# Feed-forward groups of four, a braided first tile, and a chained closing in a macaron decoder step

## The chip, the core and the metric

The kernel runs on one core of a Trainium2 chip. The metric is the device time of one execution in microseconds; a comparison uses the median of several. The kernel is written for TensorE (PE, the matrix array), VectorE (DVE), ScalarE (ACT) and SyncE (SP, which issues nearly all loads and stores); a scheduler fixes the order of the instructions on each engine beforehand, and each engine works through its own row in that order.

## What is computed

One decoder layer for 1024 prompt tokens and 64 sampled tokens, 1024 wide, all in 32-bit floats: a half-step SwiGLU block, two mixers side by side, and a second half-step SwiGLU block.

```python
def swiglu_ffn(x, w_up, w_down):
    gate, up = jnp.split(x @ w_up, 2, axis=-1)
    return (jax.nn.silu(gate) * up) @ w_down          # inner width 2816

x = x + 0.5 * rms_norm(swiglu_ffn(rms_norm(x, n1), up1, down1), n1_post)
m = parallel_mixers(rms_norm(x, mix_norm_pre), w_in, ...)   # windowed attention and gated DeltaNet
x = x + rms_norm(m, mix_norm_post)
x = x + 0.5 * rms_norm(swiglu_ffn(rms_norm(x, n2), up2, down2), n2_post)
```

## The kernel before

Activations lie transposed: 1024 features as 8 slices (k) of 128 partitions, the 1088 tokens along the free axis in chunks of 384, 384 and 320 (chunk 0, 1, 2). Every matmul with full precision is made of three, from a high and a low half of each operand: `hi*xh + hi*xl + lo*xh` (`gemm`, lines 133 to 142). So each loaded weight, 128 x 512 in a staging buffer `raw` (4 of them), is split: ACT casts the high half (line 111), DVE subtracts it (line 112).

A feed-forward part (class `FFN`, lines 307 to 505) goes over 22 inner tiles. Chunk 2 is done plainly: `one` makes gate and up of one tile (48 matmuls) and their gated product `h`. Chunks 0 and 1 are done together by a seven-product scheme with combinations of the halves of weights (`factors`) and of inputs (`combine`): `two` makes one inner tile for both chunks with 84 matmuls of 384 columns. The inputs' pieces are `ch` and `cl`, eleven steps of `combine`, each with a 128 x 1536 subtraction on DVE (lines 261, 269).

Inner tiles come in groups of two (`G = 2`, 11 groups). When a group's tiles are done, its down products are due: for each of the 8 output slices `down_k` sums six matmuls in PSUM and adds them into `y` (DVE, line 334; for group 0 a copy by ACT, line 332). They are put behind the next group's first tile (`pay`). A down weight is loaded as two half rows of one inner tile, 4 loads a group.

The order of a part is `run`: chunk 2's first groups (pass A, 5 groups in the first part, 7 in the second), chunks 0 and 1 whole (pass B), chunk 2's other groups (6 and 4). Work of VectorE and ScalarE is spread over pass A in small steps: `take(early, 3)` after each tile makes the input of pass B (loads, sum of squares `rms`, scaling, `combine`), `take(late, 3)` the closing of chunks 0 and 1. Closing a chunk (`close1`): `post` (sum of squares over y, scaling, residual), the mixers' input xn2 (`xb`), and the sum for its norm `r2`. Each sum over partitions is one matmul with a matrix of ones into `po` (line 172), followed by a reciprocal square root on ACT (line 173) and a Newton step on ACT and DVE (lines 145 to 147).

The first group multiplies unnormed x (`xu`) and takes the norm scale r into its gated product; from the second group on the operand is the scaled `xs` (`make_xnr`). At the end chunk 2 is closed while the mixers' first units (k, v, four q) run on chunks 0 and 1: `do_kv` and `do_q` evict into slabs `SL` that lie in a pool over the feed-forward part's.

Of the kernel before, what the change touches and what calls it, by code (L numbers as in the profile page):

```python
# [13 lines left out]
P = 128  # L14
# [21 lines left out]
def body(ctx: ExitStack, tc: tile.TileContext, d):  # L36
# [84 lines left out]
    def load_w(src, name, each=None, pool=wp, tag="w"):  # L121

        r = []
        for i in range(2):
            t = raw(f"{name}_{i}")
            nc.sync.dma_start(t, src[:, 4 * i : 4 * i + 4, :])
            if each:
                each(i)
            r.append(split_w(t, *slot(f"{name}_{i}", pool, tag)))
        return r  # L130

    def gemm(ps, w, xs, c, ks=range(KT)):
# [3 lines left out]
        for i, k in enumerate(ks):  # L136
            hi, lo = w[k // 4]
            j = k % 4
            first, last = i == 0, i == len(ks) - 1
            nc.tensor.matmul(ps[:, :n], hi[:, j, :], at(xh, k), start=first, stop=False)  # L140
            nc.tensor.matmul(ps[:, :n], hi[:, j, :], at(xl, k), start=False, stop=False)  # L141
            nc.tensor.matmul(ps[:, :n], lo[:, j, :], at(xh, k), start=False, stop=last)  # L142
# [11 lines left out]
    def po_tile():  # L154
        return pp.tile([P, 512], F32, tag="po", name=uid("po"), bufs=1)

    def rms(pool, src, n, dst, scale, urgent=False):
# [13 lines left out]
        with tc.high_priority(offset=4000 if urgent else 0):  # L171
            nc.tensor.matmul(ps[:, :n], ones, one, start=True, stop=True)
# [122 lines left out]
    CUT1, CUT2 = 5, 7  # L295
    G = 2
    NG = NFF // G

# [9 lines left out]
    class FFN:  # L308


        def __init__(self, up, down, pool, tag):
            self.up, self.down, self.pool, self.tag = up, down, pool, tag
            self.y = [None] * 3
            self.due = None

        def ldd(self, f):
            src = self.down[f].rearrange("p (k m) -> p k m", m=P)
            return load_w(src, uid(f"d{self.tag}"), pool=self.pool, tag="d")

        def down_k(self, g, hs, wd, c, k):  # L320
# [14 lines left out]

        def pay(self):
            if self.due:
                self.due()
                self.due = None

        def one(self, hh, hl, wg, wu, xs, r):
# [3 lines left out]
            gemm(pg, wg, {c: xs}, c)  # L345
            gemm(pu, wu, {c: xs}, c)
# [12 lines left out]
        def pass_a(self, gs, xs, r=None, first=None, between=None):  # L359
# [3 lines left out]
            for g in gs:  # L363
                h = self.pool.tile([P, 4, width(2)], F32R, tag="big", name=f"h{self.tag}{g}")
                hs = [(h[:, 2 * i, :], h[:, 2 * i + 1, :]) for i in range(G)]
                ws = first() if first and g == 0 else None
                for i in range(G):
                    f = g * G + i
                    wg, wu = ws[i] if ws else [load_w(self.up[w * NFF + f], uid(f"u{self.tag}")) for w in range(2)]
                    self.one(*hs[i], wg, wu, xs(g), r(g) if r else None)  # L370
# [4 lines left out]

                def due(g=g, hs=hs):
                    wd = [self.ldd(g * G + i) for i in range(G)]
                    for k in range(KT):
                        self.down_k(g, hs, wd, 2, k)
                    between(g, G)  # L380

                self.due = due
# [13 lines left out]
        def factors(self, f):  # L396
# [3 lines left out]
            turn = [0]  # L400

            def full(name, src=None):
                turn[0] += 1
                t = raw(f"{n}_{name}") if turn[0] % 2 else self.pool.tile([P, 4, P], F32, tag="aq", name=f"{n}_{name}", bufs=3)
# [70 lines left out]
        def pass_b(self, cx, between):  # L475
            for g in range(NG):
                hs = []
                for i in range(G):
                    hs.append(self.two(g * G + i, cx))
                    self.pay()  # L480
                    if g == 0 and i == 0:
# [51 lines left out]
    with tc.tile_pool(name="f1", bufs=12, side="left", reuse_waits="tile") as big1, tc.tile_pool(  # L533
# [71 lines left out]
        def before(g, i):  # L605
            if g >= 1:
                take(early, 3)
# [869 lines left out]
```

## Time and profile before

| what | value |
|---|---|
| median of 3 runs (lowest to highest) | 2494.36 us (2488.65 to 2501.92) |
| profiled execution, its own time | 2494.16 us |
| its span | 2492.4 us |
| PE busy | 2415.2 us (97%), 14654 instructions |
| DVE busy | 1857.0 us (75%), 3770 instructions |
| ACT busy | 1145.1 us (46%), 2310 instructions |
| mean of the clock granted to PE | 0.988 |
| moved by DMA | 258.00 MB, mean 104 GB/s |

The profile is of one execution. The span is the time between its first and last instruction; a little of the run's time lies outside it. PE's busy time counts matmuls whose ends are modelled and which overlap, so that the distance from start to start tells its pace, not the duration in a row. PEclk is the clock granted to the array as a share of full speed; it has two levels, 1.0 (2.4 GHz) and 0.5 (1.2 GHz), and a number between them is a mean over a stretch.

### The profile page before, as it was taken

How to read it: one execution, taken by the hardware profiler on the slowest of the kernel's cores; microseconds unless marked ns; L12 is line 12 of the kernel's file. 1: busy time of each engine (PE TensorE's matmuls, PEld its weight loads, DVE VectorE, ACT ScalarE, POOL GpSimd, SP SyncE). 2: the span in 40 equal slices, each digit the busy share in tenths (PEclk: the TensorE clock that was granted, in tenths of full speed). 3: DMA queues.
4: the chain of work that ended last, by engine and by line, in shares of the span. 5: the costliest groups of instructions: out<-in, count | busy, mean ns of one | idle time of the engine just before them, and what ended most of it. 6: DMA issues, size and time to landing. Idle time of an engine off the chain costs nothing.

```text
span 2492.4 us, 39425 instructions
## 1 busy us (share of the span) xinstructions
PE 2415.2 (97%) x14654; PEld 2315.4 (93%) x14654; DVE 1857.0 (75%) x3770; ACT 1145.1 (46%) x2310; POOL 49.3 (2%) x36
## 2 busy tenths in 40 slices
PE   7889999999999899999999999999998999999997
PEld 7889999999998876898889889999998999999997
DVE  6896787787898476798687735664998687777787
ACT  6644333332565278644545333255754333333353
POOL 0000000000000000001011100000000000000000
PEclk9999999999999999999999999999999999999998
DMA  6421221221554111222112335444542121221263
GB/s 222 143 95 64 73 73 59 77 69 60 185 199 161 64 52 34 87 70 78 61 59 74 105 107 159 138 146 149 192 151 89 64 77 64 72 73 60 98 209 129
DMA packets 157457, 258.00 MB, mean 104 GB/s; under 512 B 34544, under 2 KB 61616, under 8 KB 157256
## 3 DMA queue, kind: packets, MB, share of 16 engines
q1 hardware_dynamic: 157264, 255.47, 31.2%
q8 instruction: 115, 1.88, 0.3%
q14 instruction: 78, 0.64, 0.1%
HBM read 219.43 MB, written 36.96 MB: 103 GB/s over the span
## 4 chain that ended last, share of the span: by engine, by line
PE 83%; DVE 9%; ACT 3%; DMA 3%; issue 2%; SPq 0%; DVEq 0%; ACTq 0%
PE pa L141 10%; PE pa L140 10%; PE pa L142 10%; PE pa L440 8%; PE pa L441 8%; PE pa L439 8%; PE py L328 3%; PE ph L328 3%; PE py L329 3%; PE py L330 3%; PE ph L329 3%; PE ph L330 3%; DVE t L935 1%; PE po L848 1%; DVE s L1113 1%
## 5 line engine op out<-in xcount | busy, mean ns | idle before, releaser
L440 PE MATMUL pa<-cl,h_c_s 128*128 128x384 f32 x704 | 237.6, 338 | 9.2 <-DVE cl L269 9.2
L439 PE MATMUL pa<-ch,h_c_s 128*128 128x384 f32 x704 | 236.9, 337 | 2.6 <-ACT ch L268 2.5
L441 PE MATMUL pa<-ch,l_c_s 128*128 128x384 f32 x704 | 236.9, 337 | 0.0
L445 DVE TENSOR_TENSOR t<-pa,t 128x384 f32<-128x384 f32 x308 | 168.5, 553 | 44.4 <-PE pa L441 43.6
L440 PE MATMUL pa<-cl,h_c_a 128*128 128x384 f32 x528 | 176.7, 335 | 3.2 <-DVE cl L269 3.2
L439 PE MATMUL pa<-ch,h_c_a 128*128 128x384 f32 x528 | 176.8, 335 | 0.0
L441 PE MATMUL pa<-ch,l_c_a 128*128 128x384 f32 x528 | 176.6, 334 | 0.0
L440 PEld LDWEIGHTS pa<-cl,h_c_s 128*128 128x128 f32 x704 | 133.9, 190 | 9.9 <-DVE cl L269 9.9
L439 PEld LDWEIGHTS pa<-ch,h_c_s 128*128 128x128 f32 x704 | 133.4, 190 | 3.4 <-ACT ch L268 3.0
L441 PEld LDWEIGHTS pa<-ch,l_c_s 128*128 128x128 f32 x704 | 133.8, 190 | 0.0
L111 ACT CAST h_c_a<-r_c_a 128x512 fp32r<-128x512 f32 x132 | 81.9, 620 | 109.1 <-PE pa L440 88.9
L111 ACT CAST h_db<-r_db 128x512 fp32r<-128x512 f32 x88 | 52.9, 621 | 171.0 <-PE ph L329 113.1
L140 PE MATMUL pa<-xbh,h_ga 128*128 128x384 f32 (+1 forms) x384 | 129.2, 337 | 0.0
L141 PE MATMUL pa<-xbl,h_ga 128*128 128x384 f32 (+1 forms) x384 | 129.0, 336 | 0.0
L142 PE MATMUL pa<-xbh,l_ga 128*128 128x384 f32 (+1 forms) x384 | 128.5, 335 | 0.0
L111 ACT CAST h_da<-r_da 128x512 fp32r<-128x512 f32 x88 | 53.1, 620 | 157.6 <-PE ph L329 100.6
L111 ACT CAST h_c_s<-c_s 128x512 fp32r<-128x512 f32 x132 | 81.6, 618 | 62.3 <-PE pa L440 56.7
L328 PE MATMUL py<-ha,h_da 128*128 128x384 f32 (+1 forms) x264 | 88.3, 335 | 17.0 <-ACT ha L188 9.0
L440 PEld LDWEIGHTS pa<-cl,h_c_a 128*128 128x128 f32 x528 | 99.1, 188 | 3.7 <-DVE cl L269 3.7
L439 PEld LDWEIGHTS pa<-ch,h_c_a 128*128 128x128 f32 x528 | 99.1, 188 | 0.2
L441 PEld LDWEIGHTS pa<-ch,l_c_a 128*128 128x128 f32 x528 | 99.1, 188 | 0.0
L141 PE MATMUL pa<-xbl,h_qkv 128*128 128x384 f32 (+1 forms) x288 | 97.9, 340 | 0.0
(585 smaller groups left out, 7601.3 us busy)
## 6 DMA issues: line engine op xcount, KB each, us to landing
r_c_a<-in_up_dram SPq DMA_DIRECT2D x132, 256.0 KB
r_da<-in_dn_dram SPq DMA_DIRECT2D x88, 256.0 KB
r_ub<-in_up_dram SPq DMA_DIRECT2D x88, 256.0 KB
r_db<-in_dn_dram SPq DMA_DIRECT2D x88, 256.0 KB
r_ua<-in_up_dram SPq DMA_DIRECT2D x80, 256.0 KB
c_a<-in_up_dram SPq DMA_DIRECT2D x44, 256.0 KB
r_ga<-in_win_dram SPq DMA_DIRECT2D x32, 256.0 KB
r_wo<-in_wo_dram SPq DMA_DIRECT2D x32, 256.0 KB
```

Source lines behind the costliest of these rows:

```text
L111: nc.scalar.copy(hi, full)
L140: nc.tensor.matmul(ps[:, :n], hi[:, j, :], at(xh, k), start=first, stop=False)
L141: nc.tensor.matmul(ps[:, :n], hi[:, j, :], at(xl, k), start=False, stop=False)
L142: nc.tensor.matmul(ps[:, :n], lo[:, j, :], at(xh, k), start=False, stop=last)
L328: nc.tensor.matmul(ps[:, :n], hi[:, j, :], hh, start=i == 0, stop=False)
L329: nc.tensor.matmul(ps[:, :n], hi[:, j, :], hl, start=False, stop=False)
L330: nc.tensor.matmul(ps[:, :n], lo[:, j, :], hh, start=False, stop=i == G - 1)
L439: nc.tensor.matmul(ps, wh[:, k, :], xh[:, k, :], start=k == 0, stop=False)
L440: nc.tensor.matmul(ps, wh[:, k, :], xl[:, k, :], start=False, stop=False)
L441: nc.tensor.matmul(ps, wl[:, k, :], xh[:, k, :], start=False, stop=k == 3)
L445: nc.vector.tensor_tensor(out=out, in0=ps, in1=other, op=ALU.add)
L848: nc.tensor.matmul(po[hs, tp2 * 256 : tp2 * 256 + 256], vtok[:, blk * P + hs.start : blk * P + hs.stop], ptb[:, g2 * 512 + h2 * 256 : g2 * ...
```

## The change

Groups. `GROUPS` are four tiles each (4, 4, 4, 4, 4, 2) and pass A's first stage is three groups (12 tiles) in both parts. The down weights are laid out by output slice, `[k, partition, inner tile, 128]`, so one load of 256 KB holds the four tiles of a group for one k. A group's down products are two parts of four slices each (`owe`), one behind the first tile of the next group and one behind the second (`pay`); a product sums twelve matmuls. Weights of `one` and the down weights take staging buffers by turns from `raw` and from the pool `aq` of three that `factors` had used. `take` is 3 and 3 in the first part, 4 and 2 in the second.

Start. The first tile's gate and up alternate by k (`braid`), its four weight loads alternate with the four loads of x, its sum of squares gets a high priority, and the load of `wab` (the mixers' small weights) moves behind the first part.

Closing. The units' order is k, q, q, q, q, v; their slabs come from a pool of their own (`s2c`); and the two ones matmuls of chunk 2's closing get an ordering dependency (no wait) behind the chunk-1 products of the first and the fourth unit in number (u = 0 and 3).

```diff
-    CUT1, CUT2 = 5, 7
-    G = 2
-    NG = NFF // G
+    GROUPS = [range(f, min(f + 4, NFF)) for f in range(0, NFF, 4)]
+    CUT = 3
...
+        def raw(self, name):
+            self.turn += 1
+            if self.turn % 2:
+                return raw(name)
+            return self.pool.tile([P, 4, P], F32, tag="aq", name=f"q_{name}", bufs=3)
...
+        def ldd(self, g, k):
+            fs = GROUPS[g]
+            n = uid(f"d{self.tag}")
+            s = slice(0, len(fs))
+            t = self.raw(n)
+            nc.sync.dma_start(t[:, s, :], self.down[k][:, fs[0] : fs[-1] + 1, :])
+            hi, lo = slot(n, self.pool, "d")
+            return split_w(t[:, s, :], hi[:, s, :], lo[:, s, :])
...
-            for i in range(G):
-                hi, lo = wd[i][k // 4]
-                hh, hl = hs[i]
-                j = k % 4
-                nc.tensor.matmul(ps[:, :n], hi[:, j, :], hh, start=i == 0, stop=False)
-                nc.tensor.matmul(ps[:, :n], hi[:, j, :], hl, start=False, stop=False)
-                nc.tensor.matmul(ps[:, :n], lo[:, j, :], hh, start=False, stop=i == G - 1)
+            hi, lo = wd
+            for i, (hh, hl) in enumerate(hs):
+                nc.tensor.matmul(ps[:, :n], hi[:, i, :], hh, start=i == 0, stop=False)
+                nc.tensor.matmul(ps[:, :n], hi[:, i, :], hl, start=False, stop=False)
+                nc.tensor.matmul(ps[:, :n], lo[:, i, :], hh, start=False, stop=i == len(hs) - 1)
...
+        def owe(self, g, cs, hs, between):
+            def part(j):
+                for k in range(4 * j, 4 * j + 4):
+                    wd = self.ldd(g, k)
+                    for c in cs:
+                        self.down_k(g, [t[c] for t in hs], wd, c, k)
+                between(g, 4 + j)
+            self.due += [lambda: part(0), lambda: part(1)]
...
-            gemm(pg, wg, {c: xs}, c)
-            gemm(pu, wu, {c: xs}, c)
+            if braid:
+                for k in range(KT):
+                    for ps, w in ((pg, wg), (pu, wu)):
+                        gemm(ps, w, {c: xs}, c, ks=(k,), ends=(k == 0, k == KT - 1))
...
         def first():
...
+            for i in range(2):
+                for w in range(2):
+                    t = raw(f"w0{w}{i}")
+                    nc.sync.dma_start(t, d["up1"][w * NFF][:, 4 * i : 4 * i + 4, :])
+                    load_x(2, 4 * i + 2 * w)
+                    ws.append(split_w(t, *slot(f"w0{w}{i}")))
             nc.sync.dma_start(eye1, d["eye1"])
             drain(make_xn(x0[2], xu, V_N1A))
-            drain(stat(2))
+            with tc.high_priority(offset=20000):
+                drain(stat(2))
...
         drain(close1(2))
+        behind = sums[-2:]
...
-    SL = [(s2a if k < 11 else s2b).tile([P, NT], F32, tag=f"s{k}", name=f"s{k}") for k in range(16)]
+    SL = [(s2c if k in (0, 2, 3, 4, 5) else s2a).tile([P, NT], F32, tag=f"s{k}", name=f"s{k}") for k in range(16)]
...
-        for u in range(6):
+        for u in (0, 2, 3, 4, 5, 1):
...
+                if c == 1 and u in (0, 3):
+                    tc.add_manual_dep(behind[u // 3].ins, mm.ins.name, NOSYNC, reason="behind products that are ready")
...
-        take(early, 3)
-        if (g, i) == (CUT2 - 1, G - 1):
+        take(early, 4)
+        if (g, i) == (CUT - 1, 3):
             drain(early)
...
-    f2.run(CUT2, lambda g: xn3[0], cx2, lambda: again(xd[2], hn2, r3[2]), before, lambda g, i: take(late, 3))
+    f2.run(lambda g: xn3[0], cx2, lambda: again(xd[2], hn2, r3[2]), before, lambda g, i: (g, i) != (CUT, 0) and take(late, 2))
...
-        arr["dn" + n] = np.ascontiguousarray(L0(a + "_w_down")).reshape(NFF, P, 1024)
+        arr["dn" + n] = np.ascontiguousarray(L0(a + "_w_down").reshape(NFF, P, KT, P).transpose(2, 1, 0, 3))
```

How the order moves, at three places. PE at the start, before: the last products of the second tile (its up half, in ph) and the first down products (py, ph), which need `ha`, the first group's gated product. The first down product is the array's 98th instruction.

```order
L140 MATMUL ph_285<-xuh_1_128,h_wu_1_222 128x320
L141 MATMUL ph_285<-xul_1_130,h_wu_1_222 128x320
L142 MATMUL ph_285<-xuh_1_128,l_wu_1_223 128x320
L328 MATMUL py_482<-ha_136,h_da_0_460 128x320
L328 MATMUL ph_490<-ha_136,h_da_0_460 128x320
L328 MATMUL py_498<-ha_136,h_da_0_460 128x320
```

After, the same place: in front of the first down product now stand four tiles, so that it is the 194th instruction and not the 98th.

```order
L138 MATMUL ph_457<-xuh_1_128,h_ua_1_452 128x320
L139 MATMUL ph_457<-xul_1_130,h_ua_1_452 128x320
L140 MATMUL ph_457<-xuh_1_128,l_ua_1_453 128x320
L343 MATMUL py_643<-ha_133,h_da_639 128x320
L344 MATMUL py_643<-ha_133,h_da_639 128x320
L345 MATMUL py_643<-ha_133,l_da_640 128x320
L343 MATMUL py_643<-ha_133,h_da_639 128x320
```

The down product reads the same `ha`, 96 matmuls later, and goes on in one accumulator where before it changed with each matmul. DVE at the end of pass A's first stage in the first part, before: cl are the low halves of the combined inputs, the L350 row is the last tile's gated product, the L445 row already belongs to pass B.

```order
L269 TENSOR_TENSOR cl_1364<-cf_1183,ch_1363 128x1536
L261 TENSOR_TENSOR cf_1377<-x_1_122,cf_1361 128x1536
L269 TENSOR_TENSOR cl_1371<-x_0_123,ch_1370 128x1536
L350 TENSOR_TENSOR t_113_1460<-pa_1411,t_113_1460 128x320
L269 TENSOR_TENSOR cl_1380<-cf_1361,ch_1379 128x1536
L189 TENSOR_TENSOR ha_1186<-t_113_1460,ha_1186 128x320
L269 TENSOR_TENSOR cl_1466<-x_1_122,ch_1465 128x1536
L445 TENSOR_TENSOR t_124_1559<-pa_1546,t_122_1544 128x384
```

After, L381 is the gated product of the tenth of twelve tiles, L435 and L112 prepare weights for pass B, and L349 adds down products:

```order
L272 TENSOR_TENSOR cl_1255<-cf_1082,ch_1254 128x1536
L435 TENSOR_TENSOR q_c_s_1634<-r_c_a_1632,r_c_s_1624 128x512
L272 TENSOR_TENSOR cl_1262<-x_0_123,ch_1261 128x1536
L264 TENSOR_TENSOR cf_1268<-x_1_122,cf_1252 128x1536
L272 TENSOR_TENSOR cl_1271<-cf_1252,ch_1270 128x1536
L112 TENSOR_TENSOR l_c_a_1629<-r_c_a_1620,h_c_a_1628 128x512
L381 TENSOR_TENSOR t_101_1351<-pa_1302,t_101_1351 128x320
L349 TENSOR_TENSOR ya_1_132<-py_1362,ya_1_132 128x320
L112 TENSOR_TENSOR l_c_s_1637<-r_c_s_1624,h_c_s_1636 128x512
L192 TENSOR_TENSOR ha_1085<-t_101_1351,ha_1085 128x320
```

Three cl stand ahead of the tenth tile's product, with two tiles to follow; before, two of the four shown stood behind the last tile's. PE at the closing, before: po is the sum for chunk 2's mixer norm, the products around it are those of the second unit (v).

```order
L140 MATMUL pa_8628<-xbh_1_7176,h_kvq_0_1_8624 128x384
L141 MATMUL pa_8628<-xbl_1_7178,h_kvq_0_1_8624 128x384
L142 MATMUL pa_8628<-xbh_1_7176,l_kvq_0_1_8625 128x384
L172 MATMUL po_8468<-rms_8455,eye_72 128x320
L140 MATMUL pa_8654<-xbh_0_7921,h_kvq_0_0_8618 128x384
L141 MATMUL pa_8654<-xbl_0_7923,h_kvq_0_0_8618 128x384
```

After, the same sum:

```order
L140 MATMUL pa_8573<-xbh_1_7314,l_kvq_0_1_8570 128x384
L138 MATMUL pa_8599<-xbh_0_8035,h_kvq_0_0_8563 128x384
L139 MATMUL pa_8599<-xbl_0_8037,h_kvq_0_0_8563 128x384
L175 MATMUL po_8279<-rms_8266,eye_72 128x320
L140 MATMUL pa_8599<-xbh_0_8035,l_kvq_0_0_8564 128x384
L138 MATMUL pa_8599<-xbh_0_8035,h_kvq_0_0_8563 128x384
```

It stands behind the chunk-1 products of the fifth unit in number, the fourth to be issued (a q), between matmuls of the following accumulator; the sum of chunk 2's post norm stands 125 rows ahead of it.

## Rows read from the trace of the kernel before

**Rows 1.** The page's head.

```profile
span 2492.4 us, 39425 instructions
```

**Rows 2.** A stretch: PE, PEld, DVE, ACT, POOL busy (instructions); clock, DMA share, GB/s.

```profile
550.00:600.00 50.00, 50.00 (x289) 50.00 (x288) 39.03 (x71) 17.70 (x33) 0.00 (x0) 1.00 0.23 75
```

**Rows 3.** Waits of PE: waiting line, awaited line, us in total, times, longest.

```profile
PE pa L440 <- DVE cl L269: 12.4, 4, 4.6
PE po L172 <- DVE rms L168: 9.2, 2, 6.4
PE py L328 <- ACT ha L188: 9.0, 2, 7.3
PE py L328 <- ACT h_da L111: 8.0, 1, 8.0
PE pa L140 <- ACT xuh L195: 6.4, 1, 6.4
PE pa L140 <- DVE s L661: 2.9, 1, 2.9
PE pa L439 <- ACT ch L268: 2.5, 2, 1.3
```

**Rows 4.** Stretches, as in Rows 2, behind the pause of the closing.

```profile
815.00:820.00 5.00, 1.88 (x3) 0.97 (x4) 2.04 (x6) 2.79 (x5) 0.00 (x0) 0.50 0.00 0
820.00:830.00 10.00, 10.00 (x47) 9.25 (x47) 3.77 (x21) 1.24 (x2) 0.00 (x0) 0.79 0.14 50
```

**Rows 5.** Time line of PE: start, us, engine, line, operation, output and input.

```profile
1866.51 0.31 PE L330 MATMUL ph<-hb,l_db 128*128 128x320 f32 x1
1866.66 0.31 PE L328 MATMUL py<-hb,h_db 128*128 128x320 f32 x1
...
1874.98 0.53 PE L439 MATMUL pa<-ch,h_c_s 128*128 128x384 f32 x1
1875.31 0.53 PE L440 MATMUL pa<-cl,h_c_s 128*128 128x384 f32 x1
```

**Rows 6.** Stretches, as in Rows 2, of the start.

```profile
0.00:50.00 50.00, 36.10 (x205) 34.07 (x206) 36.48 (x74) 33.79 (x72) 0.21 (x4) 0.93 0.81 266
0.00:80.20 80.20, 58.35 (x340) 55.41 (x341) 53.64 (x103) 51.35 (x108) 0.21 (x4) 0.91 0.57 188
12.00:24.00 12.00, 12.00 (x81) 11.63 (x79) 8.86 (x14) 7.55 (x17) 0.00 (x0) 1.00 0.83 286
80.20:157.00 76.80, 68.48 (x425) 66.41 (x423) 71.13 (x108) 43.33 (x82) 0.00 (x0) 0.96 0.39 125
142.50:157.00 14.50, 12.95 (x59) 12.62 (x59) 12.08 (x15) 7.40 (x16) 0.00 (x0) 0.80 0.12 37
```

**Rows 7.** Time line of ACT, columns as in Rows 5.

```profile
66.75 0.58 ACT L173 ACTIVATE r<-po,epsc 128x384 f32<-128x384 f32 x1
...
72.37 0.61 ACT L111 CAST h_da<-r_da 128x512 fp32r<-128x512 f32 x1
```

**Rows 8.** Groups by line: busy us, mean ns of one, idle before and releaser.

```profile
L112 DVE TENSOR_TENSOR l_da<-r_da,h_da 128x512 fp32r<-128x512 f32 x88 | 59.3, 690 | 29.5 <-ACT h_da L111 17.6 <-PE ph L330 11.3
...
L111 ACT CAST h_da<-r_da 128x512 fp32r<-128x512 f32 x88 | 53.1, 620 | 157.6 <-PE ph L329 100.6 <-DMA r_da<-in_dn_dram 56.5 <-ACT rms L163 0.3
...
L334 DVE TENSOR_TENSOR yb<-py,yb 128x384 f32<-128x384 f32 x80 | 44.5, 556 | 21.7 <-PE py L330 20.7
```

**Rows 9.** Time line of PE, columns as in Rows 5: the closing's two ones matmuls.

```profile
794.33 0.73 PE L172 MATMUL po<-rms,eye 128*128 128x320 f32 x2
...
815.21 1.41 PE L172 MATMUL po<-rms,eye 128*128 128x320 f32 x2 [6.37 <-DVE rms L168]
```

**Rows 10.** Time line of DVE, columns as in Rows 5.

```profile
1838.53 0.56 DVE L146 TENSOR_TENSOR rms<-rms 128x384 f32<-128x384 f32 x1 [0.20 <-ACT rms L145]
...
1874.45 1.75 DVE L269 TENSOR_TENSOR cl<-cf,ch 128x1536 fp32r<-128x1536 f32 x1
```

**Rows 11.** Stretch, as in Rows 2, behind the last matmul.

```profile
2480.00:2492.40 12.40, 0.00 (x0) 0.00 (x0) 7.99 (x18) 1.13 (x3) 0.00 (x0) 0.50 0.27 106
```

More of the change, by code (lines that the diff above doesn't have):

```diff
@@ L138, in gemm @@
             j = k % 4
[L139 removed]
+            first, last = ends[0] and i == 0, ends[1] and i == len(ks) - 1
             nc.tensor.matmul(ps[:, :n], hi[:, j, :], at(xh, k), start=first, stop=False)
             nc.tensor.matmul(ps[:, :n], hi[:, j, :], at(xl, k), start=False, stop=False)
[L142 removed]
+            mm = nc.tensor.matmul(ps[:, :n], lo[:, j, :], at(xh, k), start=False, stop=last)
+        return mm
     def newton(dst, ve, tmp):
@@ L171, in rms @@
         with tc.high_priority(offset=4000 if urgent else 0):
-            nc.tensor.matmul(ps[:, :n], ones, one, start=True, stop=True)
+            sums.append(nc.tensor.matmul(ps[:, :n], ones, one, start=True, stop=True))
         nc.scalar.activation(dst, ps[:, :n], AF.Abs_reciprocal_sqrt, scale=scale, bias=epsc)
@@ L363, in pass_a @@
             for g in gs:
[L364 to L370, printed above, removed]
+                hs = []
+                for i, f in enumerate(GROUPS[g]):
+                    if i % 2 == 0:
+                        h = self.pool.tile([P, 4, width(2)], F32R, tag="big", name=f"h{self.tag}{f}")
+                    hs.append({2: (h[:, i % 2 * 2, :], h[:, i % 2 * 2 + 1, :])})
+                    braid = first is not None and f == 0
+                    wg, wu = first() if braid else [self.ldu(w, f) for w in range(2)]
+                    self.one(*hs[i][2], wg, wu, xs(g), r(g) if r else None, braid)
                     if f == NFF - 1:
@@ L374, in pass_a @@
                     between(g, i)
[L376 to L382, printed above, removed]
+                self.owe(g, (2,), hs, between)
         def put(self, tiles, dst):
@@ L473, in two, with pass_b @@
             return {0: (h[:, 0, :], h[:, 1, :]), 1: (h[:, 2, :], h[:, 3, :])}
-        def pass_b(self, cx, between):
-            for g in range(NG):
+        def pass_b(self, cx):
+            for g, fs in enumerate(GROUPS):
                 hs = []
-                for i in range(G):
-                    hs.append(self.two(g * G + i, cx))
+                for i, f in enumerate(fs):
+                    hs.append(self.two(f, cx))
                     self.pay()
-                    if g == 0 and i == 0:
+                    if f == 1:
                         self.put(self.y[2], yd)
@@ L605, in before @@
         def before(g, i):
-            if g >= 1:
+            if g or i > 1:
                 take(early, 3)
-            if (g, i) == (CUT1 - 1, G - 1):
+            if (g, i) == (CUT - 1, 3):
                 drain(early)
-        f1.run(CUT1, xs1, cx1, lambda: again(d["x2"], hn1, r1[2]), before, lambda g, i: take(late, 3), r=lambda g: None if g else r1[2], first=first)
+        f1.run(xs1, cx1, lambda: again(d["x2"], hn1, r1[2]), before, lambda g, i: (g, i) != (CUT, 0) and take(late, 3), r=lambda g: None if g else r1[2], first=first)
         drain(late)
```

83 lines of the change are left out of this document (40 added, 43 removed).

## The prediction, made before the changed kernel ran

> **What bounds the kernel now.** I read the page's head first, then the busy time by stretches, then what the array waits for, and last single stretches of the time line. The span is 2492.4 us [rows 1]; the profiled run's own time is 2494.2, so 1.8 us lie outside it, and it stands at the median of the three runs shown (2494.4). In the middle of the feed-forward part the array starts 289 matmuls in 50.00 us and is busy for all of it, 173 ns for one with 384 columns, while VectorE works 39.03 of 50 [rows 2]. So the array's own pace sets the time there, and work taken from VectorE buys nothing. What can be won are the array's pauses. The list of its waits [rows 3] names a handful: 12.4 us in four waits for the low halves of the combined inputs (cl, the operands of the two-chunk stage), 9.2 for the column sums before a ones matmul (rms), 9.0 for the gated activations (ha), 8.0 in one wait for the cast of a down weight (h_da), 6.4 for the first operand, 2.9 for an eviction into a slab (s), 2.5 for the high halves (ch). After each longer pause the granted clock is at the lower of its two levels (0.50 is 1.2 GHz) [rows 4], where matmuls of 384 columns start 0.33 us apart [rows 5] and not 0.17.
>
> All matmuls stay (13488 in both programs), so the sum counts pauses and slow matmuls, stage by stage.
>
> **The start of the first feed-forward part.** Until 80.2 us the array does 340 matmuls [rows 6]. At the pace of the stretch 12 to 24 us (81 in 12.00, 148 ns for 320 columns) they are 50.3 us, so 29.9 are lost: 6.4 before the first, 7.3 and 7.9 in two waits [rows 3], and 8.3 in what follows these three, some 2.8 for each cold start. The 7.3 come because the first group has two tiles: its down products are due while the ones matmul for the gating scale has just run. Now four tiles go ahead of them (193 matmuls and not 97), the sum has high priority, so that wait goes. The 7.9 come from ScalarE's order: the down weights' cast stands behind a rsqrt that waits for the ones matmul and ran at 66.75, and so came only at 72.37 [rows 7]. That cast is now queued elsewhere, but the pattern stays: the second operand of the full tiles (xs) is cast behind down-weight casts and the small wab cast. Up to those loads SP's queue has 27 (first slice) and 35 (second) of 256 KB, and x whole with eye1 (4.6 MB): 11.7 and 13.8 MB. At 266 to 286 GB/s [rows 6] these are in at 41 to 52 us. The array comes to the first use at row 211, about 6.4 + 2.8 + 210 x 0.148 = 40 us, and to the second at row 251, about 46. Bounds for the stall: 0 if all is cast in time, 12 if the queue behind it starts from the slow end (the two old waits together were 15). I take 5, and one more cold start of 2.8. So the same 340 matmuls end at 50.3 + 6.4 + 2.8 + 5 + 2.8 = 67.3 and not 80.2: 13 us won.
>
> The Trainium skill ("DMA: Bandwidth & Descriptors", Specifications) puts a core's share of HBM at about 358 GB/s; by that figure the 13.8 MB would be in by 39 us, the stall gone and the gain 21, the sum 2452. The trace's 266 and 286 in the loaded stretches decide, and the sum goes by them.
>
> From 80.2 to 157 us there are 425 matmuls, about 60 of them, from 142.5 on, with 384 columns [rows 6]: 365 x 0.148 + 60 x 0.173 = 64.4, so 12.4 of 76.8 are lost, nearly all at the step to the two-chunk stage, where the pieces of the combination are late (half of the 12.4 for cl and of the 2.5 for ch [rows 3], and a cold start). Before, cl stand around and behind the last gated product of the one-chunk stage; now three, that of the second product of the two-chunk stage among them, stand ahead of the tenth tile's, and from there the array has 157 matmuls (23 us) to that product, since the stage has twelve tiles and not ten and half the adds. VectorE's rows up to these cl sum to some 97 us at the durations of [rows 8] and their like, and the array comes to its first use at row 785, near 67 + 445 x 0.148 = 133. I take 1 us left: 11 won. Bounds 6 to 12.
>
> **Down products in groups of four.** Twelve matmuls go into an output tile and not six; the adds fall from 264 to 144 for each feed-forward part, 120 x 0.556 us [rows 8] = 67 us of VectorE each. In pass B this lies beside a full array [rows 2]: 0. It adds four 256 KB loads and casts a pass (0.62 ScalarE, 0.69 VectorE [rows 8]), hidden the same way: 0. Its unknown is whether each down product now waits for its own weight, since a weight serves one output tile and not a whole inner tile, and seven staging buffers serve everything. Before, waits for down casts in pass B are nil; the one case, 8.0 us, is the start's [rows 3]. I take 0; bounds 0 to one whole load, cast and subtraction for each of 24 parts (below).
>
> Changing banks with every third matmul, which the braided first tile does on two accumulators, already happens at full pace: py and ph alternate 0.15 us apart at 320 columns [rows 5]. The Trainium skill ("TensorE: Matmul & The Clock Gate", A second HAM failure mode: psum-queue depth-cycling) reports a kernel whose clock falls and rises because it cycles through PSUM banks; by it the braid's 48 matmuls would stay at the low level, and at 0.13 us more for each (0.16 of [rows 5], at 320 of 384 columns) the sum would be 6 us higher, 2466. The trace does not agree, and the sum has 0 for it.
>
> **The closing.** Between 780 and 830 us the array waits 1.7 (ha), 6.4 (sums of chunk 2) and 2.9 (kT and q wait for slabs over the feed-forward pool), and then 1.9 of its 5 us and the next 47 matmuls run slow: 0.9 + (10.0 - 47 x 0.173) = 2.8 [rows 3, 4]. Together 13.8. Now the two ones matmuls stand behind the products of the first and the fourth unit; from one to the other are 125 matmuls, 21.7 us. Before, 20.9 us lay between the two, and VectorE's chain set the second [rows 9]; it now has the evictions of these units in between, some 3 us. So 1 to 3 are late there; the slab wait goes with the slabs' own pool. The one-chunk stage ahead of it has ten tiles and not twelve, and its last sums (xb's low half) are 2 to 3 us late too. I leave 6 with part of a cold start: 8 won. Bounds 2 to 12.
>
> **The second feed-forward part.** At its step to the two-chunk stage the loss is the other half of those waits and a cold start, 6.2 + 1.3 + 2.8 = 10.3. VectorE is nearly unbroken from the second chunk's Newton step at 1838.53 to the end of the last cl needed, 1876.2 [rows 10]: 37.7 us. In the new order 211 matmuls (31.5 us) stand between that sum's ones matmul and the first use, 217 before, and VectorE's rows from the step to that cl sum to 33, with some 4 of sums and rsqrt ahead of them. The order of the pieces is a little better, the place the same: 2 won, bounds -4 to 8. At the end the tail behind the last matmul, 12.4 us [rows 11], is the same chain of adds: 0, bounds -3 to 3.
>
> **Sum.** 2494.2 - 13 - 11 - 8 - 2 = 2460. The bounds of the terms, not all at one end, give 2444 to 2478.
>
> **Rivals.** (a) *Half comes back.* For it: the start's queue is DMA-bound and ScalarE takes its work in order; the closing stage has less array work to hide the same VectorE work. If the start gives 6, the step 8 and the closing 2, the time is 2478, up to 2482. Against it: the adds taken away free about 20 us of VectorE in just these stages.
> (b) *Everything goes.* All 29.9 - 9.2 of the start, 12.4, 13.8 and 10.3 would give 2494 - 57 = 2437. Against it: the loads' 41 to 52 us, and VectorE's 37 against 31.5.
> (c) *Down weights come late in pass B, slower than before.* Each part pays for its first weight: 256 KB at 266 GB/s (1.0 us), cast 0.62, subtraction 0.69, 2.3 us, in 12 parts in each of two passes: 55 us, 2515. It decides from 34 / 24 = 1.4 us a part. Against it: four buffers hold a whole part's weights, a tile of 84 matmuls (14.5 us) lies between parts, and VectorE has 11 of 50 us free.
> (d) *The dependency does nothing or the gains are only moved*, the stalls returning as waits of the mixers' first units for r2: within 12 us of before, about 2488.
>
> **How the numbers follow.** What a measurement can tell from no change here is 0.5%, 12.5 us, so faster means under 2482. Forecast 0.57, (a) 0.18, (b) 0.08, (d) 0.10, (c) 0.07. All of the forecast, of (b) and nearly all of (a) are faster: 0.81; (d) and the rest of (a) the same: 0.12; slower 0.07. The range 2436 to 2488 leaves (c), half of (d) and the lower half of (b) out.
>
> **What will show it.** In the profile after: no wait of 7 us for ha or h_da in the first 80 us, the 340th matmul near 67 us, a wait for xs's casts of a few us near 45; cl waits under 2 us at the first step and still about 5 at the second; the wait of po for rms under 3; pass B at 50.00 of 50 with VectorE near 35. It is wrong if pass B shows array waits on h_d casts, if the start's stall is over 12 us, or if the second step's cl wait is gone (then my count of VectorE's row is wrong).

## The result, and the profile after

The changed kernel takes 2464.59 us (median of 4 runs, 2461.62 to 2466.29) against 2493.36 (4 runs, 2488.65 to 2501.92): a ratio of 0.988, 95% interval 0.985 to 0.9909. The forecast was 2460 with a range of 2436 to 2488. The profiled run took 2461.62, with a span of 2459.8 us, 32.6 less than in [rows 1].

The page's head of the changed kernel, then its busy times. TensorE does the same work as before; VectorE has 107 us less to do.

```profile
span 2459.8 us, 39261 instructions
...
PE 2405.7 (98%) x14654; PEld 2305.9 (94%) x14654; DVE 1750.1 (71%) x3550; ACT 1147.1 (47%) x2326; POOL 49.2 (2%) x36
```

TensorE's waits in the changed kernel: waiting line, awaited line, us in total, times, longest.

```profile
PE po L175 <- DVE rms L171: 8.2, 3, 3.6
PE pa L138 <- ACT xuh L198: 6.3, 1, 6.3
PE pa L463 <- DVE cl L272: 4.7, 1, 4.7
PE pa L462 <- DVE t L468: 4.0, 9, 1.3
...
PE pa L138 <- ACT xsh L191: 1.9, 2, 1.1
```

Beside [rows 3]: the four waits for cl are one; those for ha (9.0), h_da (8.0) and the slab (2.9) are gone; the two for rms have become three of at most 3.6; the first operand's is unchanged. Two rows are new: short waits for the scaled operand (xsh), and nine for t, the sum into which VectorE adds a product of the two-chunk stage.

The closing's ones matmuls in TensorE's time line of the changed kernel:

```profile
779.49 0.91 PE L175 MATMUL po<-rms,eye 128*128 128x384 f32 x2 [3.05 <-DVE rms L171]
781.55 1.44 PE L175 MATMUL po<-rms,eye 128*128 128x320 f32 x2 [1.14 <-ACT rms L177]
...
806.77 0.78 PE L175 MATMUL po<-rms,eye 128*128 128x320 f32 x2
```

The last of them, which waited 6.37 in [rows 9], waits for nothing; an earlier one now waits 3.05.

Stretches of the changed kernel, with the columns of [rows 2].

```profile
0.00:50.00 50.00, 41.85 (x255) 39.95 (x256) 39.69 (x78) 37.57 (x76) 0.20 (x4) 1.00 0.87 292
50.00:100.00 50.00, 48.42 (x317) 46.44 (x316) 41.62 (x74) 35.95 (x73) 0.00 (x0) 1.00 0.47 149
550.00:600.00 50.00, 49.43 (x284) 48.86 (x283) 39.37 (x70) 21.32 (x39) 0.00 (x0) 1.00 0.33 99
```

Most of the two-chunk stage of the first part (pass B), before and then after:

```profile
200.00:650.00 450.00, 449.80 (x2585) 449.00 (x2583) 341.04 (x614) 157.55 (x289) 0.00 (x0) 1.00 0.23 77
200.00:650.00 450.00, 448.14 (x2570) 446.29 (x2569) 300.87 (x535) 159.78 (x296) 0.00 (x0) 1.00 0.26 80
```

In the first 50 us the array does 255 matmuls and not 205, at a granted clock of 1.00 and not 0.93 [rows 6]. From 550 to 600 us it does 284 and not 289 [rows 2]: the two-chunk stage has become a little slower, although VectorE has less to do in it.

To lay all kernels side by side I add up a loss for each stage: for every matmul of 320 or 384 columns into pa, py or ph the distance to the next start, less 146.7 or 173.3 ns, and for a sum's ones matmul (two passes) less 0.70 us. It holds pauses and slow matmuls together. "Start" runs from the first matmul to 8 us before the first product of the two-chunk stage, "step" from there to 30 us behind it, "pass B" on to its last product; "closing" begins 25 us before the first product of k and ends 30 us before the last of the units.

| kernel | median us | ratio to before, 95% | start | step 1 | pass B 1 | closing | step 2 | pass B 2 |
|---|---|---|---|---|---|---|---|---|
| before | 2493.4 | | 24.7 | 11.4 | 2.9 | 15.0 | 10.8 | 3.3 |
| after | 2464.6 | 0.985 to 0.991 | 8.7 | 1.2 | 6.0 | 8.3 | 7.3 | 6.6 |
| e1 closing on before | 2482.0 | 0.994 to 0.997 | 26.2 | 11.2 | 2.9 | 1.8 | 10.7 | 3.1 |
| e2 after, old start | 2466.8 | 0.987 to 0.991 | 9.4 | 0.3 | 6.9 | 8.3 | 7.8 | 6.2 |
| e3 after, old closing | 2485.7 | 0.994 to 0.997 | 8.9 | 1.1 | 8.9 | 27.3 | 8.2 | 6.4 |
| e4 after, no chain | 2462.7 | 0.986 to 0.989 | 8.8 | 0.3 | 5.4 | 8.2 | 7.0 | 5.9 |
| e5 10 and 12 tiles | 2469.4 | 0.989 to 0.992 | 8.8 | 12.3 | 5.0 | 1.5 | 7.0 | 7.4 |
| e6 part 2: 14 and 8 | 2455.0 | 0.983 to 0.986 | 9.3 | 0.8 | 5.9 | 7.9 | 0.1 | 5.1 |
| e7 down casts low | 2451.4 | 0.981 to 0.984 | 8.5 | 0.2 | 2.6 | 8.1 | 3.8 | 2.6 |
| e8 nine slots | 2458.1 | 0.984 to 0.987 | 8.3 | 0.2 | 2.6 | 8.8 | 8.9 | 2.7 |
| e9 before, 12 and 10 | 2499.4 | 1.001 to 1.003 | 26.6 | 2.0 | 3.0 | 20.9 | 13.8 | 3.1 |
| e10 = e7 + e6 | 2452.6 | 0.982 to 0.985 | 8.8 | 0.2 | 3.6 | 8.3 | 0.1 | 2.6 |
| e11 = e10, 11 and 11 | 2447.9 | 0.980 to 0.983 | 8.1 | 1.1 | 3.6 | 3.8 | 0.1 | 2.7 |
| e12 = e10, 10 and 12 | 2449.0 | 0.980 to 0.983 | 8.2 | 1.2 | 8.6 | 1.5 | 0.1 | 2.7 |

From before to after the six columns fall by 16.0 + 10.2 - 3.1 + 6.7 + 3.5 - 3.3 = 30.0 of the 32.6 us. The other 2.6 lie in the mixers between the units and the second part (835.1 us before, 832.5 after); that stretch took 831.4 to 840.2 us in the fourteen profiles, so nothing can be made of 2.6. The columns are of one profile for each kernel, the medians of all its runs: e2's and e3's profiles (2472.15 and 2488.51 us) are the longest of their runs, e9's (2494.49) is the shortest of ten.

### The profile page after: what moved, and what is told of

It reads as the page before. It is cut to its first block, busy times and chain, and to the rows that moved or that the text cites. A ratio compares the mean times of both kernels' runs of the same rounds, so it can differ in the third digit from the quotient of the medians.

```text
span 2459.8 us, 39261 instructions
## 1 busy us (share of the span) xinstructions
PE 2405.7 (98%) x14654; PEld 2305.9 (94%) x14654; DVE 1750.1 (71%) x3550; ACT 1147.1 (47%) x2326; POOL 49.2 (2%) x36
## 4 chain that ended last, share of the span: by engine, by line
PE 82%; DVE 9%; DMA 4%; ACT 3%; issue 2%; SPq 0%; DVEq 0%; ACTq 0%
PE pa L138 10%; PE pa L139 10%; PE pa L140 10%; PE pa L462 8%; PE pa L464 7%; PE pa L463 7%; PE py L344 3%; PE py L345 3%; PE ph L345 3%; PE ph L343 3%; PE ph L344 3%; PE py L343 3%; PE po L874 1%; DMA q_da<-in_dn_dram 1%; DVE t L961 1%
## 5 line engine op out<-in xcount | busy, mean ns | idle before, releaser
L468 DVE TENSOR_TENSOR t<-pa,t 128x384 f32<-128x384 f32 x308 | 170.1, 554 | 83.3 <-PE pa L464 82.9
L111 ACT CAST h_c_s<-q_c_s 128x512 fp32r<-128x512 f32 x132 | 82.0, 621 | 103.8 <-PE pa L463 93.3
L138 PE MATMUL pa<-xbh,h_qkv 128*128 128x384 f32 (+1 forms) x288 | 97.4, 338 | 0.0
L140 PE MATMUL pa<-xbh,l_qkv 128*128 128x384 f32 (+1 forms) x288 | 97.0, 337 | 0.0
L111 ACT CAST h_c_s<-r_c_s 128x512 fp32r<-128x512 f32 x44 | 27.4, 623 | 148.2 <-PE pa L463 133.6
```

The costliest lines, as they stand in the source:

```text
L111: nc.scalar.copy(hi, full)
L140: mm = nc.tensor.matmul(ps[:, :n], lo[:, j, :], at(xh, k), start=False, stop=last)
L468: nc.vector.tensor_tensor(out=out, in0=ps, in1=other, op=ALU.add)
```

## The experiments

**e1. The closing alone, on the kernel before.**

```diff
-    SL = [(s2a if k < 11 else s2b).tile(...) for k in range(16)]
+    SL = [(s2c if k in (0, 2, 3, 4, 5) else s2a).tile(...) for k in range(16)]
...
-        for u in range(6):
+        for u in (0, 2, 3, 4, 5, 1):
...
+                if c == 1 and u in (0, 3):
+                    tc.add_manual_dep(behind[u // 3].ins, mm.ins.name, NOSYNC, ...)
```

> The kernel before with only the closing changed: units in the order k, q, q, q, q, v, slabs in a pool of their own, the two ones matmuls chained. Theory (each stage's pauses are worth what they cost there, whatever the others do): the waits of 6.4 and 2.9 us around 809 to 820 shrink to under 3 together and the cold start with them, 6 to 8 us less than before, about 2486. Rival (the closing gains only because groups of four free VectorE there): the wait for rms stays at 5 or more, 0 to 3 us less, about 2492.

Measured: 2481.97 us, 13.4 less than before's 2495.36 in the same session, more than either number. TensorE's time line around the closing in e1: of the waits there only one of 0.45 us is left, and the ones matmuls (L176) have none.

```profile
779.80 0.81 PE L176 MATMUL po<-rms,eye 128*128 128x384 f32 x2
...
786.16 0.41 PE L332 MATMUL py<-ha,h_da 128*128 128x320 f32 x1 [0.45 <-ACT ha L192]
...
803.78 0.70 PE L176 MATMUL po<-rms,eye 128*128 128x320 f32 x2
```

The whole 13 us go; 6 to 8 were expected. The closing's change needs nothing from the groups of four.

**e2. The changed kernel with the old start.** Four tiles still stand ahead of the first down products.

```diff
-            for i in range(2):
-                for w in range(2):
+            for w in range(2):
+                for i in range(2):
...
-            with tc.high_priority(offset=20000):
-                drain(stat(2))
+            drain(stat(2))
...
-                    self.one(..., braid)
+                    self.one(..., False)
```

> The changed kernel with the start's loads and order as before: gate then up and not braided, x loaded within the gate's halves, no priority for the sum of squares, wab loaded first; groups of four stay. Theory (four tiles ahead of the down products take the 7.3 us wait away, not the braid): the first 340 matmuls end within 4 us of the changed kernel's, 2466 to 2469. Rival (the braid and the early sum carry the start's gain): waits of 6 us or more come back before 60 us, 2472 or more.

Measured: 2466.78 us, interval 0.9868 to 0.9907, which covers the changed kernel's 0.988; the start's loss is 9.4 and not 8.7, and the 341st matmul starts at 66.79 us and not at 65.47. So the gain of the start goes with the groups of four, and the braid, the load order and the early sum together are worth 1.3 us at most. The groups of four bring the four tiles and seven staging buffers in place of four; no run takes these two apart.

**e3. The changed kernel with the old closing** (e1's edit taken back).

> The changed kernel with the closing as before: units in the order k, v, q, q, q, q, slabs in the pool over the feed-forward part's, no chaining. Theory: the waits for rms and for the slab (s) come back, some 6 us more than the changed kernel, 2471. Rival (with ten tiles in the closing stage and half the adds VectorE is early enough anyway): under 2 us more, 2466. Second rival (the compressed stage makes it worse than before): 10 us or more, 2475.

Measured: 2485.67 us, 21 more than the changed kernel: the second rival. TensorE's time line of e3:

```profile
780.78 1.65 PE L175 MATMUL po<-rms,eye 128*128 128x384 f32 x2 [5.43 <-DVE rms L171]
783.58 1.44 PE L175 MATMUL po<-rms,eye 128*128 128x320 f32 x2 [1.14 <-ACT rms L177]
805.66 1.41 PE L175 MATMUL po<-rms,eye 128*128 128x320 f32 x2 [10.04 <-DVE rms L171]
809.98 0.69 PE L138 MATMUL pa<-xbh,h_kvq 128*128 128x384 f32 x1 [2.92 <-DVE s L682]
```

Where before waited 6.37 for the last sum [rows 9], e3 waits 10.04, and 5.43 for one that had been early. With ten tiles and groups of four to hide the closing, and the old order, the loss is 27.3 against before's 15.0. Taken in this order the change loses 12 there by its regrouped stage and wins 19 by its new order; taken the other way round the new order wins 13 (e1) and the regrouped stage gives 6 to 7 back (8.3 against e1's 1.8). Only the difference, 6.7, is to be seen from outside.

**e4. The changed kernel without the chain.**

```diff
-                if c == 1 and u in (0, 3):
-                    tc.add_manual_dep(behind[u // 3].ins, mm.ins.name, NOSYNC, ...)
```

> The changed kernel without the two ordering dependencies of the ones matmuls; unit order and slab pool stay. TensorE's order is then the same row by row through the whole closing and differs only behind it, in the mixers. Theory (the dependency changes nothing that the new unit order and pool do not already give): within 2 us of the changed kernel, 2463 to 2467, with the same waits for rms at the closing. Rival (the chain carries the closing's gain): 5 us more, 2470.

Measured: 2462.69 us; the closing's loss is 8.2 and not 8.3. The dependency has no effect that these runs can tell. Unit order and slab pool do the work; the two were not tried apart.

**e5. Ten tiles ahead of the first part's step, twelve behind.**

```diff
-    GROUPS = [range(f, min(f + 4, NFF)) for f in range(0, NFF, 4)]
+    GROUPS1, CUT1 = [range(0, 4), range(4, 8), range(8, 10), range(10, 14), range(14, 18), range(18, 22)], 3
```

> The changed kernel with the first part's groups 4, 4, 2 ahead of the two-chunk stage and 4, 4, 4 behind it: ten tiles first, twelve at the closing, as the kernel before had them; all else as changed. Theory (the pauses left at the closing, 3.1 and 1.2 us for po with a cold start, come from the shorter closing stage): they go, 5 to 7 us less than the changed kernel, about 2458; the step to the two-chunk stage stays free, since VectorE's rows up to cl were some 35 us ahead of the array there. Rival (the ten-tile first stage brings the cl wait of the step back): a wait of 4 to 5 us for cl near 115 us, 2463 or more.

Measured: 2469.41 us, 5 more than the changed kernel (the intervals of the two overlap, and the columns show the trade). The theory was right on the closing (8.3 to 1.5) and wrong on the step (1.2 to 12.3), which decided. TensorE's waits for cl in e5; one of the three, 4.7, is the second part's:

```profile
PE pa L464 <- DVE cl L272: 9.6, 3, 4.7
```

**e9. The kernel before with twelve tiles ahead and ten behind.**

```diff
-    CUT1, CUT2 = 5, 7
+    CUT1, CUT2 = 6, 6
```

> The kernel before with six groups of two (twelve tiles) in the first stage of both parts, and nothing else changed. Theory (the step of the first part came free in the changed kernel because its stage has twelve tiles and not ten, not because of the fewer adds): the two cl waits and the ch wait near 137 and 155 us go, 10 us won there; the closing stage of ten tiles loses some 8 again as in e3; 2488 to 2494. Rival (the halved adds took the wait away): the cl waits at the first step stay above 4 us together, 2500 or more.

Measured: 2499.37 us, slower than before (1.0012 to 1.0032). Step 1 falls from 11.4 to 2.0 with groups of two and all the adds, so the theory holds on what it was made to tell. What it won went to the closing (15.0 to 20.9) and to step 2 with its two tiles fewer (10.8 to 13.8); I had priced the first of these alone. The start's 26.6 is no more than e1's 26.2 with the same start. In sum e9's columns are only 1.3 us above before's: its profile is 4.9 us under the median of its runs. With e5: two more tiles ahead of the step take its wait away, and the fewer adds alone do not. Twelve tiles do it with either grouping, ten with neither, as long as the down weights are split early (e12 has ten tiles with a loss of 1.2 where they are not).

**e6. Fourteen tiles ahead of the second part's step, eight behind.**

```diff
+    GROUPS2, CUT2 = [range(0, 4), range(4, 8), range(8, 12), range(12, 14), range(14, 18), range(18, 22)], 4
...
-    f2.run(..., lambda g, i: (g, i) != (CUT, 0) and take(late, 2))
+    f2.run(..., lambda g, i: (g, i) != (CUT2, 0) and take(late, 3))
```

`take(early, 4)` stays; its 59 steps are then done in 15 of 20 calls, and not in 15 of 16.

> The changed kernel with the second part's groups 4, 4, 4, 2 ahead of the two-chunk stage and 4, 4 behind it (fourteen and eight tiles), 4 steps a call ahead and 3 behind. 383 matmuls, 57 us, then stand between the second chunk's ones matmul and the first cl use in place of 211. Theory (the 4.7 us cl wait and its cold start are this distance against VectorE's 37 us): they go, 6 to 7 us less, about 2458. Rival (the eight-tile stage at the end makes up for it: its sums come late and the wait before the last ones matmul and the tail grow): no gain, 2463 or more.

Measured: 2454.98 us, 9.6 less than the changed kernel; step 2 goes from 7.3 to 0.1, as the theory has it. The rest, some 2 us, is no more than medians of one kernel differ between sessions.

**e7. Down weights split at their place in the program.**

```diff
-    def split_w(full, hi, lo):
-        with tc.high_priority(offset=20000):
+    def split_w(full, hi, lo, offset=20000):
+        with tc.high_priority(offset=offset):
...
-            return split_w(t[:, s, :], hi[:, s, :], lo[:, s, :])
+            return split_w(t[:, s, :], hi[:, s, :], lo[:, s, :], 0)
```

> The changed kernel with the cast and subtraction of the down weights at their place in the program instead of the high priority; weights of gate and up as before. Theory (the waits of pa for t in the two-chunk stages, 0.2 to 1.3 us each and some 7 us a run, come from a down weight's cast that stands ahead in ScalarE's and VectorE's rows while its load has not landed): they shrink, 3 to 6 us less, about 2460. Rival (the casts then come too late for the down products): waits of py or ph for h_d appear, the same or up to 20 us more.

Measured: 2451.42 us, 13 less than the changed kernel, interval 0.9813 to 0.9842. Here is how the new waits come about. In the changed kernel ScalarE stands for 1.62 and 0.86 us before the casts of two down weights whose loads have not landed (its time line):

```profile
382.29 0.62 ACT L111 CAST h_da<-q_da 128x512 fp32r<-128x512 f32 x1 [1.62 <-DMA q_da<-in_dn_dram]
...
384.82 0.62 ACT L111 CAST h_da<-q_da 128x512 fp32r<-128x512 f32 x1 [0.86 <-DMA q_da<-in_dn_dram]
```

VectorE (next) reaches the subtractions of these weights in its own order, and the add that empties an accumulator (L468) stands behind five splits, 4.4 us after the one before it:

```profile
382.25 0.56 DVE L468 TENSOR_TENSOR t<-pa,t 128x384 f32<-128x384 f32 x1 [0.85 <-PE pa L464]
...
384.16 0.68 DVE L112 TENSOR_TENSOR l_da<-r_da,h_da 128x512 fp32r<-128x512 f32 x1
385.47 0.69 DVE L112 TENSOR_TENSOR l_da<-q_da,h_da 128x512 fp32r<-128x512 f32 x1 [0.62 <-ACT h_da L111]
386.08 0.68 DVE L112 TENSOR_TENSOR l_c_a<-r_c_a,h_c_a 128x512 fp32r<-128x512 f32 x1
386.69 0.55 DVE L468 TENSOR_TENSOR t<-pa,t 128x384 f32<-128x384 f32 x1
```

and TensorE, which has three accumulators for these products, waits for it:

```profile
387.29 0.44 PE L462 MATMUL pa<-ch,h_c_s 128*128 128x384 f32 x1 [0.74 <-DVE t L468]
```

In the changed kernel eight of the nine waits for t stand behind such a cluster of five splits, three of them of down weights. In e7's VectorE row for the same place, the adds stand between the splits, 1.7 us (from the second of the pair) and 2.3 us apart, and no wait for t of 0.2 us or more is left in the first part's pass B:

```profile
380.32 1.02 DVE L468 TENSOR_TENSOR t<-pa,t 128x384 f32<-128x384 f32 x2 [0.85 <-PE pa L464]
381.26 0.68 DVE L112 TENSOR_TENSOR l_c_a<-r_c_a,h_c_a 128x512 fp32r<-128x512 f32 x1
381.86 0.69 DVE L112 TENSOR_TENSOR l_da<-q_da,h_da 128x512 fp32r<-128x512 f32 x1
382.46 0.55 DVE L468 TENSOR_TENSOR t<-pa,t 128x384 f32<-128x384 f32 x1
382.93 0.69 DVE L112 TENSOR_TENSOR l_da<-r_da,h_da 128x512 fp32r<-128x512 f32 x1
383.52 0.69 DVE L112 TENSOR_TENSOR l_c_a<-r_c_a,h_c_a 128x512 fp32r<-128x512 f32 x1
384.13 0.69 DVE L112 TENSOR_TENSOR l_da<-q_da,h_da 128x512 fp32r<-128x512 f32 x1
384.73 0.55 DVE L468 TENSOR_TENSOR t<-pa,t 128x384 f32<-128x384 f32 x1
```

The same stretch as in [rows 2] in e7 is full again, 289 matmuls:

```profile
550.00:600.00 50.00, 50.00 (x289) 50.00 (x288) 39.13 (x70) 21.54 (x39) 0.00 (x0) 1.00 0.32 95
```

Pass B gets back to 2.6 in both parts, and step 2 falls from 7.3 to 3.8, which I had not expected: the early down splits had also stood in VectorE's row between the pieces of the combination (four from 1797.8 to 1803.3 us in the changed kernel, none there in e7). The rival's waits for down weights come to 0.3 us.

**e8. Nine staging buffers, three pairs for split down weights.**

```diff
-            return self.pool.tile([P, 4, P], F32, tag="aq", name=f"q_{name}", bufs=3)
+            return self.pool.tile([P, 4, P], F32, tag="aq", name=f"q_{name}", bufs=5)
...
-        name="d1", bufs=4
+        name="d1", bufs=3
```

> The changed kernel with nine staging buffers in place of seven (five in aq) and three in place of four pairs for split down weights. Theory (the loads of the down weights are issued late because a staging buffer is not free; with two more they land before their casts): the waits of pa for t go, 3 to 6 us less, about 2460. Rival (three pairs do not hold a part of four weights, so the cast of the fourth waits for the array and holds ScalarE): waits of py or ph for h_d or more waits for t, 5 to 30 us more.

Measured: 2458.09 us; pass B goes to 2.6 and 2.7, step 2 stays at 8.9. It fits the other half of the explanation: with the splits' early place kept and two more buffers to load into, the same waits go. What ScalarE's casts of down weights wait for their loads in the first part's pass B (160 to 660 us) tells the two apart; before, changed kernel, e7, e8:

```profile
ACT h_da L111 <- DMA r_da<-in_dn_dram: 54.6, 32, 3.8
ACT h_da L111 <- DMA q_da<-in_dn_dram: 10.4, 9, 2.2
ACT h_da L111 <- DMA q_da<-in_dn_dram: 9.7, 9, 1.8
ACT h_da L111 <- DMA r_da<-in_dn_dram: 0.8, 3, 0.3
```

e7 leaves the loads as late as they were and moves the splits; e8 still has clusters of five, at a slightly different place (4.1 to 4.3 us from add to add), but the loads are in time, and no wait of TensorE for t is left there. Before, the casts waited longer still and it cost nothing: inside a tile at most two splits stood between two adds. What fits all four is that a late load and a cluster of splits in the row have to meet. How much of e8's gain is the loads', and how much the cluster's place or the three pairs in place of four, is not shown.

**e10, e11, e12. Down casts low, fourteen and eight tiles, and the first part's tiles split 12 and 10, 11 and 11, 10 and 12.** The first diff is e11's, the second e12's.

```diff
+    GROUPS1, CUT1 = [range(0, 4), range(4, 8), range(8, 11), range(11, 15), range(15, 19), range(19, 22)], 3
...
+    GROUPS1, CUT1 = [range(0, 4), range(4, 8), range(8, 10), range(10, 14), range(14, 18), range(18, 22)], 3
```

> e7 and e6 together: down weights' casts at their place in the program, second part's groups 4, 4, 4, 2 and 4, 4. Theory: e7 has already taken most of the second step's wait away, so the fourteen tiles add only what was left there, the 1.4 us wait and its like, 2 to 4 us; 2447 to 2450. Rival (both gains add up fully): 9 us less than e7, 2442. Second rival (the eight-tile end costs it back): 2452 or more.

Measured: 2452.64 us, as much as e7: the second rival's number, but not its reason. Step 2 went as foretold (3.8 to 0.1), and at the end the last sum waits 2.5 us and not 3.6; the mixers took 836.6 us and not 831.4.

> e10 with the first part's groups 4, 4, 3 and 4, 4, 3 (eleven and eleven tiles). Theory (the waits left at the closing, 2.7 and 1.2 us with a cold start, shrink with a tile more in the closing stage, while the first step has room since the down casts stand behind the combination now): 3 to 5 us less than e10. Rival (the first step's cl wait returns as in e5): the same as e10 or up to 5 more.

Measured: 2447.92 us, 4.7 less than e10: the theory. The closing goes from 8.3 to 3.8, step 1 from 0.2 to 1.1.

> e10 with the first part's groups 4, 4, 2 and 4, 4, 4 (ten and twelve tiles). Theory: the closing is free of waits as in e5 (5 us less), the first step pays less than the 7 us of waits in e5, since VectorE's row has the combination ahead of the down weights: 0 to 4 us less than e10. Rival: the first step's waits come back in full, 4 to 6 us more than e10.

Measured: 2448.99 us, 3.7 less than e10, though the runs of the two overlap: the theory's side. The closing is free (1.5) and step 1 costs 1.2, but one wait of 3.6 us for t stands in pass B behind it:

```profile
PE pa L463 <- DVE t L469: 3.6, 1, 3.6
```

e11 is the fastest kernel, 0.9814 of before (0.98 to 0.9829); e12's interval covers it. The changed kernel's (0.985 to 0.9909) lies above both.

## Why the prediction was right, and where it was not

**The start: 13 foretold.** The 341st matmul starts at 65.47 and not at 80.23, 14.8 us earlier; 67.3 was foretold. The pauses came where I had put them, at the first and second use of xs (1.13 and 0.73 us near 42 and 49), but with two more they sum to 3.2 and not to 5. The granted clock stayed at 1.00 through them, to 100 us, and behind them the matmuls start 0.15 us apart again, so the second cold start of 2.8 in my sum was one too many:

```profile
42.17 0.56 PE L138 MATMUL pa<-xsh,h_ua 128*128 128x320 f32 x2 [1.13 <-ACT xsh L191]
42.58 0.31 PE L345 MATMUL ph<-ha,l_da 128*128 128x320 f32 x1
42.73 0.30 PE L343 MATMUL py<-ha,h_da 128*128 128x320 f32 x1
...
49.07 0.71 PE L138 MATMUL pa<-xsh,h_ua 128*128 128x320 f32 x3 [0.73 <-ACT xsh L191]
```

The loads moved at 292 GB/s over the first 50 us, faster than the 266 and 286 that I took from the old trace. The Trainium skill's 358 ("DMA: Bandwidth & Descriptors", Specifications) is no ceiling here: from 6 to 12 us the loads ran at 373. As a pace for the whole it was too high, and the stall that it would have taken away was there. On the braid's changing banks the run agrees with the old trace and not with what the Trainium skill reports ("TensorE: Matmul & The Clock Gate", A second HAM failure mode: psum-queue depth-cycling): both kernels do 19 matmuls by 12 us, and then the braid goes on from bank to bank 0.14 us apart. Two rows of TensorE's time line and a stretch of the changed kernel:

```profile
13.50 0.31 PE L140 MATMUL pa<-xuh,l_w 128*128 128x320 f32 x1
13.64 0.31 PE L138 MATMUL py<-xuh,h_w 128*128 128x320 f32 x1
```

```profile
6.00:12.00 6.00, 5.71 (x19) 5.03 (x20) 4.97 (x9) 5.91 (x15) 0.00 (x0) 1.00 1.02 373
```

**Step 1: 11 foretold, 10.2 measured.** The size holds; of the two reasons I gave, twelve tiles and half the adds, e9 shows that the first is enough and e5 that the second is not. I had summed VectorE's row at 97 us and set it against an array that arrived at 133. By that sum ten tiles would have done too; e5 shows that they don't (12.3), and e12 that they do (1.2) once the down weights are split at their place. So the sum left out what the row's order puts ahead of the last pieces.

**Down products in pass B: 0 foretold, 6.4 lost** (3.1 and 3.3). This is the step that failed. "In pass B this lies beside a full array [rows 2]: 0." counted VectorE's load and not its order. I had looked for the cost where rival (c) has it, at py and ph waiting for h_d; none is there. The late weight held the queue in which the accumulators' adds stand, and e7 and e8 each take the loss away. Of the marks that I gave for pass B, 50.00 of 50 for the array failed (49.43), while VectorE near 35 of 50 held: 300.87 of 450 us from 200 to 650 is 33 of 50. In stretches of 50 us there it runs from 28.05 to 39.37. So VectorE had room, and the array waited for it all the same. In the whole run VectorE's work fell by 107 us and not by twice 67.

**The closing: 8 foretold, 6.7 measured, of two errors that cancel.** The new order is worth 13 us by itself and 19 beside the ten-tile stage (e1, e3); the regrouped stage costs 12 with the old order and 6 to 7 with the new, for which I had 2 to 3. The wait of 3.05 for rms lies at a sum of 384 columns, chunk 0's or 1's, and not at chunk 2's second sum, where I had put 1 to 3. Rival (d)'s first half, that the dependency does nothing, is true (e4), and yet nothing of the gain is lost with it.

**Step 2: 2 foretold, 3.5 measured.** The wait of 4.7 for cl stayed, as said. That the distance between the ones matmul and the use of cl decides it is shown by e6; e7 adds that part of VectorE's row in between could be moved.

**The end: 0 foretold.** The stretch behind the last matmul is as long as in [rows 11], 12.5 us and 12.4, with the same 18 instructions of VectorE; the wait before the last sum grew from 2.8 to 3.6:

```profile
2447.30:2459.80 12.50, 0.00 (x0) 0.00 (x0) 7.99 (x18) 1.30 (x3) 0.00 (x0) 0.50 0.27 105
```

So 34 were foretold and 32.6 came, 30.0 of them in the stages. That the total came so near is partly luck: pass B's loss of 6.4 was made up by the start and step 2, which gave more than I had counted, and by the 2.6 in the mixers. Rival (a) had the right kind of event at the closing, where up to 12 us are given back; the loss in pass B stands in no rival as it came about.

Open: why the ten-tile closing stage with the old order costs more with groups of four (27.3, e3) than with groups of two (20.9, e9). Both have a wait of 10.0 for chunk 2's second sum and one of 2.9 for the slab; e3 has the 5.43 for a 384-column sum besides.

## What to carry to other kernels

Where the order on an engine is fixed beforehand, a cast of data that may land late is a gate for all that stands behind it: keep such casts at the place where they are needed, or load earlier, and look for the price at the engine that waits for what stands behind. A stage that hides other work has a size; when tiles are moved from one side of a step to the other, price both sides, since a net gain can be two large terms. Take a compound change apart even when its total is as foretold.

## What the hardware showed unasked

The granted clock can fall where TensorE's row shows no wait. In e2, 1.4 us behind the end of sixteen matmuls of 16 columns, which took 1.96 us, products of 384 columns begin to start 0.32 us apart, and they do so until 1451 us; in e7 the same program stretch, 8.73 us earlier, stayed at full clock. TensorE's rows in e2 and in e7, then the 26 us from the same place in e2 and in e7 (in the columns of [rows 2]):

```profile
1434.20 1.96 PE L1244 MATMUL py<-mq,s 128*128 128x16 f32 x16
1425.47 1.96 PE L1242 MATMUL py<-mq,s 128*128 128x16 f32 x16
```

```profile
1434.00:1460.00 26.00, 26.00 (x106) 19.10 (x106) 9.68 (x15) 10.82 (x16) 1.90 (x1) 0.74 0.21 67
```

```profile
1425.27:1451.27 26.00, 26.00 (x142) 22.03 (x142) 10.86 (x17) 11.36 (x17) 4.44 (x2) 1.00 0.41 132
```

TensorE is busy for all 26 us in both, with 106 matmuls in the one and 142 in the other. The clock goes with the spread of 831 to 840 us in the mixers: the mean granted clock of that stretch reads 1.00 in the seven shortest profiles of it (831.4 to 834.5 us) and 0.99 in the seven longest (834.5 to 840.2). Why it falls in one kernel and not in another was not tested. And the slow first matmuls of a run do not show in the column of the granted clock: from 6 to 12 us it reads 1.00 in the changed kernel, with 19 matmuls in 5.71 us.
